# A mixer's small weights loaded into another slot and earlier in the queue, and one exponential placed behind another

## The chip, the cores and the metric

The kernel runs on one core of one Trainium2 chip. The time is that of one whole execution on the device, in microseconds, as the median of several runs; lower is better. The core's engines are TensorE (PE, matrix products), VectorE (DVE), ScalarE (ACT), GpSimd (POOL) and SyncE (SP), which here issues nearly all loads. Each works through its own list of instructions in order and waits on semaphores for the others.

## What is computed

A decoder trunk of two layers on 256 tokens of width 1024. Each layer is a feed-forward with half a step, a mixer, and a second feed-forward; before each stands a root-mean-square norm with its own gain vector. The mixer runs a state-space branch and a gated delta-rule branch on the same input. Cut to what this case touches:

```python
for l in range(DEPTH):
    h = h + 0.5 * swiglu(rms_norm(h, ffn1_norm[l]), ffn1_w_in[l], ffn1_w_out[l])
    u = rms_norm(h, mix_norm[l])
    (z_s, xbc, dt_s, qkv, z_d, b_d, a_d, gate_s, gate_d) = jnp.split(u @ w_in[l], split_points, axis=-1)
    ...
    h = h + merged @ w_out[l]
    h = h + 0.5 * swiglu(rms_norm(h, ffn2_norm[l]), ffn2_w_in[l], ffn2_w_out[l])

dt = jax.nn.softplus(dt_raw + dt_bias)          # state-space branch, 32 heads
a = -jnp.exp(a_log)
beta = jax.nn.sigmoid(b_raw)                    # delta-rule branch, 8 heads
g = -jnp.exp(a_log) * jax.nn.softplus(a_raw + dt_bias)
```

The 48 columns of `w_in` that give `dt_s`, `a_d` and `b_d` are the mixer's small weights. `softplus(x)` is worked out as `max(x, 0) + log(1 + exp(-|x|))`, with the logarithm as a polynomial, so that two exponentials occur in this place: `exp(a_log)` and `exp(-|x|)`.

## The kernel before, in words

**Weights.** All large weights stream through the core as tiles of 128 x 1024 floats (512 KB). A tile is loaded by SyncE into `wraw` (five buffers), and `prep` splits it into a high part `whi` (ScalarE, `act`, line 68) and the rest `wlo` (VectorE, `tt`, line 71), five buffers each. Every product is then three TensorE passes: high by high, high by low, low by high. `take` hands out the next split tile and runs the loads and the splits ahead of it. A split waits until TensorE has done with the tile five before it.

**The order.** The program is written in the order of use. A scheduler puts the instructions of each engine into a list; `tc.issue_after(x)` holds an instruction back in that list until x has been placed, and `state["last"]` is the weight load issued last. `ORDER` lists the units of the mixer: `z` are the products for the gate z_s, `s` the steps of the small scalars, `M` the masks, and so on. `z_unit(0)` comes ahead of the list, and `z20 s z10` begin it. `z_unit` sums in two PSUM banks, one for each half of the tokens (tiles named t), and ScalarE takes each bank off as `yz`.

**Where the mixer begins.** While the feed-forward's last products run, `norm_in` normalises the tokens: `rms_chain` makes `hn` (VectorE, with the gain vector `nw`), TensorE turns it (`hnT`, line 282), and ScalarE and VectorE write it, split, into `uW`. `norm_vec(i)` loads the gain vector of norm i into the single buffer `nw` (line 215). It is called for the next norm before a mixer begins, so this load has to wait until the `hn` of the present norm have read the old vector.

**The small ones.** `mixer` then loads `lp` (convolution weights and two norms, one row for each partition, line 596), `rp` (biases and `a_log`, broadcast, line 598) and `wsr`, the small weights (128 x 8 x 48 floats, line 600). `wsr` lies in `s2`, a pool of nine buffers of 2 KB per partition, through which nearly all temporary tiles of the kernel go in turn. It is split into `wsc` (lines 68 and 71). `scalars`, step one: sixteen narrow matmuls (`psm`, lines 656 to 659), the result copied to `smT` by ScalarE, turned by TensorE (`pst`, line 664), read back as `pvs`, and then the softplus on `scr` by VectorE with ScalarE's tanh and exponential; `ea` is `exp(a_log)`, and `la` their product. Step two multiplies `la` into running sums (`psr`).

**The other slots.** `y0` to `y3` are four slots of 4 KB per partition. In a feed-forward each holds one `wsum`, a sum of two weight tiles, and they are used up one after the other; the fourth, `y3`, is split for the last time ahead of the five last weight tiles. In the mixer `y3` holds `dN` (written by the masks, `M`), and later one of the `yz`.

**Tables.** ScalarE's silu and its exponential need different tables. A table load (ACT_TABLE_LOAD) stands wherever the function changes from one set to another.

Of the kernel before, what the change touches and what calls it, by code (L numbers as in the profile page):

```python
# [7 lines left out]
F32 = mybir.dt.float32  # L8
F32R = mybir.dt.float32r
I32 = mybir.dt.int32  # L10
AF = mybir.ActivationFunctionType
ALU = mybir.AluOpType
# [4 lines left out]
P = 128  # L17
# [5 lines left out]
KT = D // P  # L23
# [3 lines left out]
RPW = 112  # L27
# [26 lines left out]
def trunk_kernel(ctx, tc, x, wst, wsm, norms, lpar, rpar, cst, out):  # L54
    nc = tc.nc
    V, A, G, PE = nc.vector, nc.scalar, nc.gpsimd, nc.tensor

    cpool = ctx.enter_context(tc.tile_pool(name="cpool", bufs=1))
    wpool = ctx.enter_context(tc.tile_pool(name="wpool", bufs=1))
    slots = ctx.enter_context(tc.tile_pool(name="slots", bufs=1))  # L60
    s2 = ctx.enter_context(tc.tile_pool(name="s2", bufs=9))
# [5 lines left out]
    def act(o, i, func=AF.Copy, **kw):  # L67
        return A.activation(out=o, in_=i, func=func, **kw)  # L68

    def tt(o, a, b, op):  # L70
        return V.tensor_tensor(out=o, in0=a, in1=b, op=op)  # L71

    def stt(o, a, s, b, op0, op1):
        return V.scalar_tensor_tensor(out=o, in0=a, scalar=s, in1=b, op0=op0, op1=op1)

    def ts(o, a, s1, op0, sc2=None, op1=None):
        if op1 is None:
            return V.tensor_scalar(out=o, in0=a, scalar1=s1, scalar2=None, op0=op0)
        return V.tensor_scalar(out=o, in0=a, scalar1=s1, scalar2=sc2, op0=op0, op1=op1)
# [7 lines left out]
    def trb(name):  # L87
        return trp.tile([P, 512], F32, tag="tr", name=name)
# [4 lines left out]
    def small(shape, name, bufs=2):  # L93
        return sm.tile(shape, F32, tag=name, name=name, bufs=bufs)
# [54 lines left out]
    state = {"loaded": 0, "prepped": 0, "taken": 0, "last": None, "hold": False, "behind": {}, "late": {}, "first": 0, "turns": {}, "first_chunk": False, "cap": n_forms}  # L149
# [62 lines left out]
    def norm_vec(i):  # L212
        nw = cpool.tile([P, D], F32, tag="nw", name="nw")
        with tc.issue_after(state["last"].ins):
            nc.sync.dma_start(nw[:], norms[i].partition_broadcast(P))
        return [nw[:, n * 512 : (n + 1) * 512] for n in range(2)]
# [375 lines left out]

    def mixer(l, nxt):
        with tc.issue_after(state["last"].ins):
            lp = cpool.tile([P, LPW], F32, tag="lp", name="lp")
            nc.sync.dma_start(lp[:], lpar[l])
            rp = cpool.tile([P, RPW], F32, tag="rp", name="rp")
            nc.sync.dma_start(rp[:], rpar[l].partition_broadcast(P))
            wsr = s2.tile([P, KT, 48], F32, tag="s2", name="wsr")
            nc.sync.dma_start(wsr[:], wsm[l])  # L600
        snw = lp[:, 240:256]
        dnw = lp[:, 256:257]
        alog = rp[:, 40:80]
# [47 lines left out]
        def scalars():  # L651
            psm = trb("psm")
            for kt in range(KT):
                both = wsc[:, kt].rearrange("p o c -> p (o c)")
                if kt < KT - 1:
                    PE.matmul(psm[0:96, 0:S], both, uTh[:, kt, :], start=kt == 0, stop=False)
                PE.matmul(psm[0:48, 0:S], wsc[:, kt, 0], uTl[:, kt, :], start=False, stop=False)
                if kt == KT - 1:
                    PE.matmul(psm[0:96, 0:S], both, uTh[:, kt, :], start=False, stop=True)
            smT = s2.tile([96, S], F32, tag="s2", name="smT")  # L660
            act(smT[:], psm[0:96, 0:S])
            pst = trb("pst")
            for t in range(2):
                PE.transpose(pst[:, t * 96 : (t + 1) * 96], smT[:, t * P : (t + 1) * P], ident[0:96, 0:96])
            pv2 = pst[:, 0:192].rearrange("p (t o c) -> p t o c", t=2, o=2)
            pvs = small([P, 2, 48], "pvs", 1)
            pv = pvs[:]
            act(pv, pv2[:, :, 1])
            tt(pv, pv2[:, :, 0], pv, ALU.add)
            scr = s2.tile([P, 5, 2, 40], F32, tag="s2", name="scr")  # L670
            xb, ax, z, s_, q_ = (scr[:, i] for i in range(5))
            tt(xb, pv[:, :, 0:40], rp[:, None, 0:40].to_broadcast([P, 2, 40]), ALU.add)
            act(dq[:, :, 8:16], pv[:, :, 40:48], AF.Tanh, scale=0.5)
            ts(dq[:, :, 8:16], dq[:, :, 8:16], 0.5, ALU.mult, 0.5, ALU.add)
            ea = small([P, 40], "ea", 1)
            with tc.issue_after(state["input"][0].ins):
                act(ea[:], alog, AF.Exp)
            stt(ax, xb, -1.0, xb, ALU.mult, ALU.max)
            act(z, ax, AF.Exp, scale=-1.0)
            ts(s_, z, 2.0, ALU.add)  # L680
            V.reciprocal(out=s_, in_=s_)
            tt(s_, s_, z, ALU.mult)
            tt(q_, s_, s_, ALU.mult)
            ts(z, q_, 1.0 / 15.0, ALU.mult)
            for d_ in (13.0, 11.0, 9.0, 7.0, 5.0, 3.0):
                stt(z, z, 1.0 / d_, q_, ALU.add, ALU.mult)
            stt(z, z, 1.0, s_, ALU.add, ALU.mult)
            ts(ax, xb, 0.0, ALU.max)
            stt(sp[:], z, 2.0, ax, ALU.mult, ALU.add)
            stt(la[:], sp[:], -1.0, ea[:, None, :].to_broadcast([P, 2, 40]), ALU.mult, ALU.mult)  # L690
            yield
            psr = trb("psr")
            for t in range(2):
                PE.matmul(psr[0:40, t * 256 : (t + 1) * 256], la[:, t, :], UU, start=True, stop=True)
            pr = psr[:].rearrange("p (t c) -> p t c", t=2)
            V.tensor_copy(rows[0:32], pr[0:32, :, 0:P])
            V.tensor_copy(rows[32:40], pr[32:40, :, P : 2 * P])
            nc.sync.dma_start(rdram[:], rows[:].rearrange("p t c -> p (t c)"))
            pac = trb("pac")
            for t in range(2):  # L700
                PE.transpose(pac[:, t * 40 : (t + 1) * 40], rows[:, t, :], ident[0:40, 0:40])
            V.tensor_copy(ac[:], pac[:, 0:80].rearrange("p (t c) -> p t c", t=2))
            V.tensor_copy(dq[:, :, 0:8], ac[:, :, 32:40])
            yield
            psp = trb("psp")
            for c in range(4):
                PE.matmul(psp[:, c * 16 : (c + 1) * 16], SEL[c % 2], dq[:, c // 2, :], start=True, stop=True)
            for a in range(2):
                V.tensor_copy(
                    pq[64 * a : 64 * a + 64].rearrange("p k h c -> p c k h"),  # L710
                    psp[64 * a : 64 * a + 64, 0:64].rearrange("p (c k h a) -> p c k h a", c=4, k=2, h=4)[:, :, :, :, a],
                )
# [484 lines left out]
        def dn_branch():  # L1197
            ps = branch("d", 4, dn_T)
            m = tg[1]
            for t in range(2):  # L1200
                for n in range(2):
                    sl = slice(n * 512, (n + 1) * 512)
                    stt(m[:, t, sl], m[:, t, sl], 1.0, ps[t][n][:], ALU.add, ALU.mult)

        sc, inv, rc = scalars(), invert(), recur()
        units = {"k": k_unit, "q": q_unit, "v": v_unit}
        rests, heads = {}, {}
# [73 lines left out]
    norm_first(nw0)  # L1281
    for l in range(DEPTH):
        ffn(norm_vec(3 * l + 1))
        mixer(l, norm_vec(3 * l + 2))
        add = ffn(norm_vec(3 * l + 3) if l + 1 < DEPTH else None)
    nw = norm_vec(3 * DEPTH)
    for t in range(2):
# [11 lines left out]
        z = small([P, 2], "zz")  # L1299
# [139 lines left out]
```

## Time and profile before

| | |
|---|---|
| median of three runs | 1545.27 us (1545.19, 1545.27, 1546.01) |
| the profiled execution | 1543.84 us |
| its span, first to last instruction | 1542.1 us |
| busy TensorE, VectorE, ScalarE, GpSimd | 1525.1, 1229.8, 949.8, 82.6 us |
| read from memory | 297.72 MB |
| granted TensorE clock over the span | 0.999 |

The profile is of one execution. Times in its rows count from the first instruction. A row of the timeline gives start, duration, engine, line, operation, output and inputs, shapes and count, and in brackets how long the engine had stood idle just before and who ended that. A row of the chain of waits gives start, duration and the work that the end of the program hung on at that time. Rows of one tile give the duration's least, middle and greatest value in ns. Matmuls overlap, so a row of 0.39 us does not keep TensorE for 0.39 us: what counts is the distance between two starts.

### The profile page before, as it was taken

Reading aid. Unit: us, or ns where it says so; the run is one execution under the profiler, and the core shown is the slowest. Engines: PE = TensorE matmul, PEld = TensorE weight load, DVE = VectorE, ACT = ScalarE, POOL = GpSimd, SP = SyncE. Lnnn points to the kernel's source line nnn. Section 1 sums busy time; section 2 is a strip of 40 time slices with the busy share of each in tenths; the row PEclk is TensorE's granted clock in tenths of the full one; section 3 lists DMA queues with packets and bytes.
Section 4 is the critical chain, followed back from the end, with each engine's and each line's share of the span. In section 5 each row is a group of like instructions: output and inputs, shape, how many; then the busy total and the mean of one; then the engine's idle time right before and its main releaser. Section 6 shows DMA issues by size and latency. Waiting matters only on the chain.

```text
span 1542.1 us, 29082 instructions
## 1 busy us (share of the span) xinstructions
PE 1525.1 (99%) x11473; PEld 1385.3 (90%) x11473; DVE 1229.8 (80%) x1859; ACT 949.8 (62%) x1536; POOL 82.6 (5%) x92
## 2 busy tenths in 40 slices
PE   8999999999999999999999999999999999999998
PEld 7999879999988888999899998899998888899997
DVE  5878768967899766789778887689579996678886
ACT  5656667766665645566555566776756666455565
POOL 0000010000000000000100012010000000000010
PEclk9999999999999999999999999999999999999999
DMA  7687765553565556577866687566346555556775
GB/s 272 187 266 227 232 223 174 183 164 112 180 209 172 157 174 191 184 252 217 264 221 227 204 254 238 182 196 186 117 137 204 180 167 187 175 179 191 250 241 156
DMA packets 98831, 305.73 MB, mean 198 GB/s; under 512 B 22837, under 2 KB 23813, under 8 KB 97670
## 3 DMA queue, kind: packets, MB, share of 16 engines
q1 hardware_dynamic: 93796, 290.95, 57.1%
q0 software_dynamic: 4608, 12.58, 5.0%
q8 instruction: 90, 1.47, 0.4%
q14 instruction: 47, 0.39, 0.1%
q10 hardware_dynamic: 290, 0.33, 0.1%
HBM read 297.72 MB, written 1.92 MB: 194 GB/s over the span
## 4 chain that ended last, share of the span: by engine, by line
PE 90%; DVE 3%; ACT 3%; DMA 2%; issue 1%; POOL 0%; SPq 0%; POOLq 0%; ACTq 0%; DVEq 0%
PE fc L346 10%; PE fc L340 9%; PE fc L345 9%; PE t L366 9%; PE o L337 4%; PE o L336 4%; PE o L335 4%; PE f L366 3%; PE b L337 3%; PE b L335 3%; PE b L336 3%; PE p L336 2%; PE p L335 2%; PE p L337 2%; PE xs L340 1%; PE xs L345 1%
## 5 line engine op out<-in xcount | busy, mean ns | idle before, releaser
L71 DVE TENSOR_TENSOR wlo<-wraw,whi 128x1024 fp32r<-128x1024 f32 x488 | 592.2, 1222 | 189.9 <-ACT whi L68 175.4
L68 ACT ACTIVATE whi<-wraw 128x1024 fp32r<-128x1024 f32 x488 | 511.4, 1059 | 266.8 <-PE fc L345 87.3
L346 PE MATMUL fc<-uW,wlo 128*128 128x256 f32 x1280 | 354.9, 277 | 0.0
L340 PE MATMUL fc<-uW,whi 128*128 128x256 f32 x1280 | 354.1, 277 | 0.0
L345 PE MATMUL fc<-uW,whi 128*128 128x256 f32 x1260 | 348.3, 276 | 0.0
L340 PEld LDWEIGHTS fc<-uW,whi 128*128 128x128 f32 x1280 | 240.5, 188 | 0.8
L346 PEld LDWEIGHTS fc<-uW,wlo 128*128 128x128 f32 x1280 | 240.5, 188 | 0.0
L345 PEld LDWEIGHTS fc<-uW,whi 128*128 128x128 f32 x1260 | 236.5, 188 | 0.8
L366 PE MATMUL t<-whi,uW 128*128 128x512 f32 x512 | 165.4, 397 | 0.0
L366 PEld LDWEIGHTS t<-whi,uW 128*128 128x128 f32 x512 | 95.9, 188 | 21.6 <-issue 1.3
L68 ACT ACTIVATE whi<-wsum 128x1024 fp32r<-128x1024 f32 x64 | 68.0, 1062 | 58.7 <-PE fc L345 32.3
L366 PE MATMUL t<-wlo,uW 128*128 128x512 f32 x256 | 100.1, 392 | 0.0
L71 DVE TENSOR_TENSOR wlo<-wsum,whi 128x1024 fp32r<-128x1024 f32 x64 | 78.2, 1222 | 8.3 <-ACT whi L68 5.9
L335 PE MATMUL b<-whi,bh 128*128 128x512 f32 x192 | 76.1, 398 | 0.3 <-ACT bh L68 0.2
L336 PE MATMUL b<-wlo,bh 128*128 128x512 f32 x192 | 75.0, 390 | 0.0
L337 PE MATMUL b<-whi,bl 128*128 128x512 f32 x192 | 74.3, 394 | 0.3 <-DVE bl L71 0.3
L340 PE MATMUL xs<-uW,whi 128*128 128x256 f32 x256 | 72.8, 284 | 0.0
L346 PE MATMUL xs<-uW,wlo 128*128 128x256 f32 x256 | 71.4, 279 | 0.0
L345 PE MATMUL xs<-uW,whi 128*128 128x256 f32 x254 | 70.5, 278 | 0.0
L335 PE MATMUL o<-whi,gh 128*128 128x512 f32 (+1 forms) x160 | 62.0, 388 | 0.0
L337 PE MATMUL o<-whi,gl 128*128 128x512 f32 (+1 forms) x160 | 61.8, 386 | 0.0
L336 PE MATMUL o<-wlo,gh 128*128 128x512 f32 (+1 forms) x160 | 61.7, 386 | 0.0
(337 smaller groups left out, 3301.2 us busy)
## 6 DMA issues: line engine op xcount, KB each, us to landing
wraw<-in_wst_dram SPq DMA_DIRECT2D x504, 512.0 KB, 4.8
wsum<-in_wst_dram SPq DMA_DIRECT2D x16, 512.0 KB, 7.3
wsum<-in_wst_dram POOLq DMA_DIRECT2D x16, 512.0 KB, 8.6
dc<-rdram SPq DMA_DIRECT2D x8, 1024.0 KB, 8.6
nw<-in_norms_dram SPq DMA_DIRECT2D x6, 512.0 KB, 5.3
h<-u POOLq DMA_DIRECT2D x12, 256.0 KB, 6.4
gb<-rdram SPq DMA_DIRECT2D x8, 256.0 KB, 6.1
h<-in_x_dram SPq DMA_DIRECT2D x4, 256.0 KB, 3.7
```

Of the source, the lines that this page charges most:

```text
L68: return A.activation(out=o, in_=i, func=func, **kw)
L71: return V.tensor_tensor(out=o, in0=a, in1=b, op=op)
L335: PE.matmul(ps, lh, rh, start=start, stop=False)
L336: PE.matmul(ps, lh, rl, start=False, stop=False)
L337: return PE.matmul(ps, ll, rh, start=False, stop=stop)
L340: PE.matmul(ps, wh, mh, start=start, stop=False)
L345: PE.matmul(ps, wh, ml, start=False, stop=False)
L346: PE.matmul(ps, wl, mh, start=False, stop=stop)
L366: ins = PE.matmul(ps[t][:], st, mv, start=k0 == 0 and j == 0, stop=k0 == KT - 2 and j == 5)
```

## The change

`wsr` gets the slot `y3` and its load becomes the first of the four; `rp` and `lp` follow; the vector of the next norm is loaded after them, inside `mixer`, instead of ahead of them. The exponential of `a_log` loses its tie to the beginning of the mixer and is tied behind the exponential of the softplus.

```diff
     def mixer(l, nxt):
         with tc.issue_after(state["last"].ins):
+            wsr = slots.tile([P, KT, 48], F32, tag="y3", name="wsr")
+            nc.sync.dma_start(wsr[:], wsm[l])
+            rp = cpool.tile([P, RPW], F32, tag="rp", name="rp")
+            nc.sync.dma_start(rp[:], rpar[l].partition_broadcast(P))
             lp = cpool.tile([P, LPW], F32, tag="lp", name="lp")
             nc.sync.dma_start(lp[:], lpar[l])
-            rp = cpool.tile([P, RPW], F32, tag="rp", name="rp")
-            nc.sync.dma_start(rp[:], rpar[l].partition_broadcast(P))
-            wsr = s2.tile([P, KT, 48], F32, tag="s2", name="wsr")
-            nc.sync.dma_start(wsr[:], wsm[l])
+        nxt = norm_vec(nxt)
...
             ea = small([P, 40], "ea", 1)
-            with tc.issue_after(state["input"][0].ins):
+            stt(ax, xb, -1.0, xb, ALU.mult, ALU.max)
+            with tc.issue_after(act(z, ax, AF.Exp, scale=-1.0).ins):
                 act(ea[:], alog, AF.Exp)
-            stt(ax, xb, -1.0, xb, ALU.mult, ALU.max)
-            act(z, ax, AF.Exp, scale=-1.0)
...
     for l in range(DEPTH):
         ffn(norm_vec(3 * l + 1))
-        mixer(l, norm_vec(3 * l + 2))
+        mixer(l, 3 * l + 2)
```

What it moves is the same in both mixers. On TensorE and GpSimd the order stays as it was. SyncE's list at the beginning of the first mixer, between the weight loads issued during the feed-forward and the eleven that follow (the norm's vector is nw):

```order
 L171 DMA wraw<-in_wst_dram 128x1024 x28
-L596 DMA lp<-in_lpar_dram 128x257
+L596 DMA wsr<-in_wsm_dram 128x384
+L598 DMA rp<-in_rpar_dram 128x112
+L600 DMA lp<-in_lpar_dram 128x257
 L215 DMA nw<-in_norms_dram 128x1024
-L598 DMA rp<-in_rpar_dram 128x112
-L600 DMA wsr<-in_wsm_dram 128x384
 L171 DMA wraw<-in_wst_dram 128x1024 x11
```

The load of wsr goes from behind nw to the front, that of lp from the front to just ahead of nw. ScalarE's list in the same place, from the normalised input (uW) to the second bank of the first z unit (t_2180 and t_2181 are its two banks):

```order
 L68 ACTIVATE uW<-hnT 128x4x128 x2
+L68 ACTIVATE wsc<-wsr 128x8x48
 L68 ACTIVATE yz<-t_2180 128x512
-L68 ACTIVATE whi<-wraw 128x1024
-L68 ACTIVATE wsc<-wsr 128x8x48
-L68 ACTIVATE whi<-wraw 128x1024
-L68 ACT_TABLE_LOAD
-L68 ACTIVATE ea<-rp 128x40
-L68 ACTIVATE whi<-wraw 128x1024
-L68 ACT_TABLE_LOAD
+L68 ACTIVATE whi<-wraw 128x1024 x3
 L68 ACTIVATE yz<-t_2181 128x512
```

The split of the small weights has moved ahead of one yz and one whi, and ea has left with both its table loads; it now stands behind the exponential of the softplus. VectorE's list, from the same uW to the first step of the softplus:

```order
 L71 TENSOR_TENSOR uW<-hnT,uW 128x4x128 x2
-L71 TENSOR_TENSOR wlo<-wraw,whi 128x1024 x2
 L71 TENSOR_TENSOR wsc<-wsr,wsc 128x8x48
-L71 TENSOR_TENSOR wlo<-wraw,whi 128x1024 x5
+L71 TENSOR_TENSOR wlo<-wraw,whi 128x1024 x7
 L71 TENSOR_TENSOR pvs<-pst,pvs 128x96
```

wsc has moved ahead of two wlo.

## The prediction

> **What bounds the kernel now.** I read the page's busy table and its chain of waits first, then the chain cut to the first mixer's opening, then TensorE's rows there beside the same rows of the second mixer.
>
> ```profile
> PE 1525.1 (99%) x11473; PEld 1385.3 (90%) x11473; DVE 1229.8 (80%) x1859; ACT 949.8 (62%) x1536; POOL 82.6 (5%) x92
> PE 90%; DVE 3%; ACT 3%; DMA 2%; issue 1%; POOL 0%; SPq 0%; POOLq 0%; ACTq 0%; DVEq 0%
> ```
>
> TensorE carries nine tenths of the chain. A step on another engine is worth only the time for which TensorE stands still because of it. The chain names the opening of the first mixer, which is where the change works:
>
> ```profile
> 195.68 6.14 DMA wsr<-in_wsm_dram
> ...
> 202.27 1.04 ACT whi L68
> 203.33 1.28 ACT L68
> ...
> 207.73 2.84 ACT whi L68 x3
> 210.57 0.27 ACT smT L68
> ...
> 210.88 0.38 PE pst L664 x2
> ```
>
> Read as a story: the load of the small weights (wsr) lands at 201.82, ScalarE had been waiting for it, then works off whi tiles and table loads, reaches smT late, and TensorE's transpose pst waits for smT. That is 15.2 us of chain (195.68 to 210.88), but not 15.2 us of loss: TensorE multiplied nearly all that time. The loss is read from TensorE's own rows, first mixer and then second:
>
> ```profile
> 209.45 0.28 PE L659 MATMUL psm<-uW,wsc 128*96 128x256 f32 x1
> ...
> 210.02 0.40 PE L366 MATMUL t<-whi,uW 128*128 128x512 f32 x1
> 210.88 0.38 PE L664 MATMUL pst<-cs,smT 96*128 96x96 f32 x2 [0.46 <-ACT smT L68]
> ...
> 971.60 0.40 PE L366 MATMUL t<-whi,uW 128*128 128x512 f32 x1
> 971.84 0.33 PE L664 MATMUL pst<-cs,smT 96*128 96x96 f32 x2
> ```
>
> In the first mixer pst starts 0.86 us after the matmul ahead of it, in the second 0.24 us, which is the ordinary spacing. So the stall is 0.86 - 0.24 = **0.62 us, once in the program**. The ScalarE rows say why only once:
>
> ```profile
> 201.84 0.53 ACT L68 ACTIVATE wsc<-wsr 128x384 fp32r<-128x384 f32 x1 [2.42 <-DMA wsr<-in_wsm_dram]
> ...
> 210.47 0.36 ACT L68 ACTIVATE smT<-psm 96x256 f32<-96x256 f32 x1
> ...
> 962.11 0.52 ACT L68 ACTIVATE wsc<-wsr 128x384 fp32r<-128x384 f32 x1 [1.11 <-DMA wsr<-in_wsm_dram]
> ...
> 971.35 0.38 ACT L68 ACTIVATE smT<-psm 96x256 f32<-96x256 f32 x1 [0.51 <-PE psm L659]
> ```
>
> In the second mixer ScalarE waited 1.11 us for wsr instead of 2.42, was 1.31 us earlier, and then itself stood 0.51 us waiting for psm. The second mixer thus shows what the first looks like with wsr only a little earlier.
>
> **The change part by part.** *The loads.* SyncE's rows in the first mixer, its wait for hn, and the times to landing of lp and, last, of wsr:
>
> ```profile
> 192.88 0.42 SPq L596 DMA_DIRECT2D lp<-in_lpar_dram  x1
> 194.77 0.33 SPq L215 DMA_DIRECT2D nw<-in_norms_dram  x1
> 195.14 0.43 SPq L598 DMA_DIRECT2D rp<-in_rpar_dram  x1
> 195.68 0.38 SPq L600 DMA_DIRECT2D wsr<-in_wsm_dram  x1
> ...
> SPq L215 <- DVE hn L74: 1.4, 1, 1.4
> ...
> DMA to landing us min/median/max: 4.1/4.3/4.5
> ...
> DMA to landing us min/median/max: 4.6/5.4/6.1
> ```
>
> Today nw waits on SyncE until 194.77 (its tile is still read by hn), and rp and wsr stand behind it. The change gives wsr the place of lp, at about 192.9, with nothing that waits in front. Its landing is bounded by 4.1 us (lp, from this very place) and 6.1 us (wsr behind the 512 KB of nw). I take 4.5 us, nearer lp, since the place is lp's and wsr is only half as large again (384 against 257 floats per partition): landing at 197.4, bounds 197.0 and 199.0, against 201.82 now. nw still leaves at 194.77 or shortly after, since it is hn that holds it. The weight loads behind then leave about 1 us earlier, as rp and wsr no longer stand between. lp leaves about 1 us later and is first read here:
>
> ```profile
> L68 ACT ACTIVATE ca<-kk,lp x16: 457/462/530, 238.2 to 1024.7; 128x256 f32<-128x256 f32 x16
> ```
>
> At 238.2 us, 40 us after it lands: no cost. If that cover were gone, the cost would be the 1 us.
>
> *The slot.* y3's former tenant, the fourth wsum, is worked off in the feed-forward before the last five weight tiles; its next tenant, dN, is written after the masks' loads. Neither holds anything. The tiles that follow wsr in s2 now take a slot that came free one tenant earlier, so their waits can only shorten. I cost both at zero.
>
> *wsc moved forward.* This is the one part that can hurt. ScalarE and VectorE now do wsc ahead of the yz and whi, and ahead of the two wlo, that used to precede it. Should wsr be late, these wait. Prices of wsc and of a wlo, with the two points at which TensorE needs the two wlo:
>
> ```profile
> L68 ACT ACTIVATE wsc<-wsr x2: 524/526/527, 201.8 to 962.1; 128x384 fp32r<-128x384 f32 x2
> L71 DVE TENSOR_TENSOR wsc<-wsr,wsc x2: 559/559/559, 202.4 to 962.7; 128x384 fp32r<-128x384 f32 x2
> ...
> 199.46 1.23 DVE L71 TENSOR_TENSOR wlo<-wraw,whi 128x1024 fp32r<-128x1024 f32 x1 [0.99 <-ACT whi L68]
> ...
> 202.47 0.39 PE L366 MATMUL t<-wlo,uW 128*128 128x512 f32 x1
> ...
> 203.84 0.39 PE L366 MATMUL t<-wlo,uW 128*128 128x512 f32 x1
> ```
>
> With landing at 197.4, wsc ends on ScalarE at 197.9 and on VectorE at 198.5; the first wlo ends at 199.7 and the second, two wlo after wsc, at about 201.0. TensorE reads them at 202.47 and 203.84. The slack is some 2.7 us, so wsr may take up to 4.5 + 2.7 = 7.2 us. The longest wsr seen took 6.1. Cost: zero.
>
> *The exponential.* ea moves behind the exponential of z, where the right table is in place. Two table loads of 1.28 us go per mixer, four in all, 5.1 us of ScalarE, and ScalarE stops waiting 2.42 and 1.11 us for wsr. What remains is that ScalarE, which reached smT at 210.47, 0.74 us after psm was done (209.45 + 0.28), reaches it early, so the 0.62 us stall goes. In the second mixer the same gain falls into ScalarE's idle time.
>
> ```profile
> 203.33 1.28 ACT L68 ACT_TABLE_LOAD   x1
> 204.63 0.24 ACT L68 ACTIVATE ea<-rp 128x40 f32<-128x40 f32 x1
> ...
> 220.18 0.24 DVE L74 SCALAR_TENSOR_TENSOR la<-sp,ea 128x80 f32<-128x80 f32 x1
> ```
>
> ea costs 0.24 us and is read at 220.18 only; behind z (ScalarE at 213.93 today) it still has some 6 us. If that cover were gone it would cost 0.24 us each time.
>
> The Trainium skill, in "ScalarE: Activation LUTs", section "What ACT_TABLE_LOAD costs", has a switch at 1283 ns for the load and about 1380 ns for a drain, 2.66 us together. The load agrees with the 1.28 us row; no drain of that size shows around it here, as ea starts 1.30 us after the load started. By the page ScalarE would gain 10.6 us instead of 5.1, and the sum of TensorE's time below would be the same, while the rival of freed ScalarE time would be larger.
>
> *The sum.* 0.62 us in the first mixer, 0 in the second. The profiled execution took 1543.84 us, 1542.1 of it the span; less 0.62 that is 1543.2. The median shown lies 1.43 us above that execution; carried over, 1545.27 - 0.62 = **1544.65 us**, 0.04% faster. About 0.2% (3.1 us) can be told from no change, so this counts as no change.
>
> **The rivals.** *Nothing is left of it.* The two mixers as wholes, from the first matmul of one to the feed-forward's first:
>
> ```profile
> 190.50 4.12 PE t L366 x18
> ...
> 597.10 4.12 PE f L366 x18
> ...
> 952.08 4.12 PE t L366 x18
> ...
> 1359.00 4.12 PE f L366 x18
> ```
>
> The first takes 406.60 us with the stall, the second 406.92 without it. A gain of 0.62 us is thus within what later stretches give and take; eaten up, the time is 1545.3. Against it: every engine downstream is fed by the same TensorE order, so that a shift has no reason to be lost.
>
> *Freed ScalarE time is worth more.* If ScalarE set the pace from here on, its four table loads (5.1 us) and its waits for wsr (2.42 + 1.11) would come off: 8.6 us, 1536.6. For it speaks that the chain runs through ScalarE for over 5 us in the rows quoted first; against it that ScalarE is busy 62% and that the second mixer turned 1.31 us of such time into 0.51 us of waiting and none of TensorE's. Something above 3.1 us would need a stall that these rows do not show.
>
> The page on ScalarE named above would add four drains of 1.38 us to this rival: 14.1 us and 1531.1; the row of 1.30 us speaks against that.
>
> *wsr lands late and stops TensorE: slower.* Place: wsc at the head of ScalarE and VectorE, with the two wlo behind it; it decides from 7.2 us to landing. The worst landing of another 512 KB load from this queue, nw, is in this row:
>
> ```profile
> DMA to landing us min/median/max: 3.6/5.3/9.5
> ```
>
> At 9.5 us each mixer would stand 2.3 us: 2 x 2.3 - 0.6 = 4.0 us, 1549.3. Against it: wsr is 192 KB, its longest is 6.1, and ahead of it stand the same weight loads that let lp land within 4.5.
>
> **How the numbers follow.** The stall goes and the gain stays: 0.62. Nothing is left: 0.20. Freed ScalarE time: 0.10. wsr late: 0.08. The first two lie within 0.2%, so 0.82 for no change, 0.10 faster, 0.08 slower. The range covers the first two with the scatter of the runs (1545.19 to 1546.01, and 1543.84 under the profile), which reaches some 1.4 us to either side, and leaves out most of the two others: 1542.5 to 1547.0.
>
> **What would show it.** Right: wsr issued near 192.9 and 954.4 us, landing in under 7 us; wsc on ScalarE just after uW; smT waiting for psm in both mixers; pst 0.24 us behind its neighbour in both; two table loads fewer per mixer; the feed-forward after the first mixer starting 0.6 us earlier, the second mixer of unchanged length. Wrong: a gap of TensorE at the first wlo of the second z unit (wsr late), a mixer shorter by more than 1 us (freed ScalarE time matters somewhere I did not see), or a new stall far behind, at the masks or the decays.

## The result, and the profile after

The changed kernel took 1542.88 us in the median of 17 runs, the kernel before, beside it, 1545.19 us (17 runs): a ratio of 0.9985, 95% interval 0.9978 to 0.9992. That is 2.3 us or 0.15% faster, inside the 0.2% that the prediction called no change, and inside its range. But the forecast gain was 0.62 us. Two more comparisons, below, gave 0.9997 (0.9989 to 1.0006) and 0.9988 (0.9979 to 0.9997); the mean of the three is 0.9990, some 1.5 us. The question left by the result is thus the size.

The page of the changed kernel, its span and its chain by engine:

```profile
span 1539.7 us, 29072 instructions
PE 89%; DVE 4%; ACT 2%; DMA 2%; issue 1%; SPq 1%; POOL 0%; POOLq 0%; ACTq 0%; DVEq 0%
```

Nothing in these shares tells of the change; the opening of the mixers does. First SyncE's rows, then ScalarE's, then TensorE's, of the first mixer after the change (line numbers behind the mixer's loads are one higher):

```profile
191.94 0.43 SPq L596 DMA_DIRECT2D wsr<-in_wsm_dram  x1
192.41 0.42 SPq L598 DMA_DIRECT2D rp<-in_rpar_dram  x1
192.88 0.43 SPq L600 DMA_DIRECT2D lp<-in_lpar_dram  x1
193.83 0.33 SPq L215 DMA_DIRECT2D nw<-in_norms_dram  x1
```

```profile
197.00 0.53 ACT L68 ACTIVATE wsc<-wsr 128x384 fp32r<-128x384 f32 x1 [1.33 <-DMA wsr<-in_wsm_dram]
197.43 0.58 ACT L68 ACTIVATE yz<-t 128x512 f32<-128x512 f32 x1
...
206.99 1.06 ACT L68 ACTIVATE whi<-wraw 128x1024 fp32r<-128x1024 f32 x1 [0.27 <-PE t L366]
208.83 0.38 ACT L68 ACTIVATE smT<-psm 96x256 f32<-96x256 f32 x1 [0.78 <-PE psm L660]
...
210.50 1.28 ACT L68 ACT_TABLE_LOAD   x1
211.79 0.27 ACT L68 ACTIVATE scr<-scr 128x80 f32<-128x80 f32 x1
211.97 0.22 ACT L68 ACTIVATE ea<-rp 128x40 f32<-128x40 f32 x1
```

```profile
209.09 0.40 PE L366 MATMUL t<-whi,uW 128*128 128x512 f32 x1
209.32 0.33 PE L665 MATMUL pst<-cs,smT 96*128 96x96 f32 x2
```

wsr leaves as soon as the weight loads ahead of it have left, at 191.94 where 192.9 was forecast (all rows of this execution come 0.9 us earlier, see below), lands 5.0 us later (forecast 4.5, bounds 4.1 and 6.1), and ScalarE now stands 0.78 us idle before smT, waiting for psm, where it had come late. pst starts 0.23 us after its neighbour: the stall of 0.62 us is gone, and ea runs at once behind scr with no table load of its own. In the second mixer pst had no stall before and has none now. So the mechanism did what was forecast. That leaves 1.7 us of the 2.4 between the spans of these two executions, 1542.1 and 1539.7 us, unexplained by it, and TensorE's rows show where they lie: 0.9 us in the first 15 us of the program, where nothing was changed, 0.2 us elsewhere in the first mixer and 0.6 us in the second. At the start TensorE's matmuls of 512 columns follow one another every 0.43 us, later every 0.23; the faster spacing begins near 15.2 us before the change and near 13.3 after it, which makes up the 0.9 us.

### The profile page after: what moved, and what is told of

It is laid out like the page before. It is cut to its first block, busy times and chain, and to the rows that moved or that the text cites. A ratio compares the mean times of both kernels' runs of the same rounds, so it can differ in the third digit from the quotient of the medians.

```text
span 1539.7 us, 29072 instructions
## 1 busy us (share of the span) xinstructions
PE 1522.8 (99%) x11473; PEld 1384.4 (90%) x11473; DVE 1229.7 (80%) x1859; ACT 944.8 (61%) x1532; POOL 81.8 (5%) x92
## 4 chain that ended last, share of the span: by engine, by line
PE 89%; DVE 4%; ACT 2%; DMA 2%; issue 1%; SPq 1%; POOL 0%; POOLq 0%; ACTq 0%; DVEq 0%
PE fc L346 10%; PE fc L340 9%; PE fc L345 9%; PE t L366 9%; PE o L337 4%; PE o L335 4%; PE o L336 4%; PE f L366 3%; PE b L335 3%; PE b L337 3%; PE b L336 3%; PE p L336 2%; PE p L337 2%; PE p L335 2%; PE xs L345 1%; PE xs L340 1%
```

## The experiments

Theory A: only the stall of 0.62 us counts, the rest is scatter. Theory B: the change has a second gain of about 1.7 us. The first four kernels ran on one chip: the two kernels again, and each half of the change alone.

**The kernel before, unchanged.**

> The kernel before, unchanged, timed against itself, to see what the comparison itself can tell. Both theories: ratio 1.000 within 0.0007 (about 1 us). Trace: the stall ahead of pst in the first mixer is there again (0.86 us between its start and the start ahead), none in the second (0.24). Theory A (only the stall matters; all else between the first two traces was scatter): TensorE's slower stretches and its slow start of up to 15 us lie elsewhere than in the first trace, by some tenths of a us each. Theory B (the change has a second gain of some 1.7 us): the differences to the changed kernel's trace at the start and in the second mixer come back in the same places.

Ratio 1.0002 (0.9993 to 1.0010). But the stall was another one. ScalarE's wait for wsr and TensorE's pst in the first mixer of this execution:

```profile
202.09 0.52 ACT L68 ACTIVATE wsc<-wsr 128x384 fp32r<-128x384 f32 x1 [3.66 <-DMA wsr<-in_wsm_dram]
```

```profile
209.03 0.40 PE L366 MATMUL t<-whi,uW 128*128 128x512 f32 x1
211.13 0.38 PE L664 MATMUL pst<-cs,smT 96*128 96x96 f32 x2 [1.71 <-ACT smT L68]
```

The distance is 2.10 us instead of 0.86, so the stall is 1.86 us, three times that of the first profile. wsr took 7.4 us to land instead of 6.1, ScalarE waited 1.24 us longer, and the stall is 1.24 us longer. The same kernel, in another execution: neither theory had foreseen this.

**The changed kernel again.**

> The changed kernel once more, beside the others on one chip. Theory A: 0.6 to 0.7 us under the kernel before (ratio 0.9996). Theory B: 2.3 us under it (0.9985). Trace: pst 0.24 us behind its neighbour in both mixers, wsr landing 5 us after its issue.

Ratio 0.9997 (0.9989 to 1.0006): too wide to part 0.62 from 1.5 us, but it holds no 2.3. pst stood 0.23 us behind its neighbour in both mixers.

**The loads alone.** The changed kernel with the old place of the exponential:

```diff
-            stt(ax, xb, -1.0, xb, ALU.mult, ALU.max)
-            with tc.issue_after(act(z, ax, AF.Exp, scale=-1.0).ins):
+            with tc.issue_after(state["input"][0].ins):
                 act(ea[:], alog, AF.Exp)
+            stt(ax, xb, -1.0, xb, ALU.mult, ALU.max)
+            act(z, ax, AF.Exp, scale=-1.0)
```

> The changed loads alone, with the exponential of a_log tied as before: its two table loads then stand right behind wsc, ahead of the first yz and of three whi (2 x 1.28 + 0.24 = 2.8 us more on ScalarE at that place). Theory A: the stall ahead of pst goes (-0.62 in the first mixer), but the second wlo of the second z unit ends about 0.3 us after TensorE wants it, in both mixers: sum about 0 (-0.62 + 2 x 0.3). Theory B: the second gain hangs on the loads or on the freed ScalarE time; 1 us or more faster if on the loads.

Ratio 0.9992 (0.9983 to 1.0001). The stall at pst is gone in both mixers (0.23), and the small new one is there in the first mixer, in TensorE's rows at the second wlo of the second z unit:

```profile
203.97 0.62 PE L366 MATMUL t<-whi,uW 128*128 128x512 f32 x2
204.64 0.50 PE L366 MATMUL t<-wlo,uW 128*128 128x512 f32 x1
204.98 0.62 PE L366 MATMUL t<-whi,uW 128*128 128x512 f32 x2
```

The row of two starts at 203.97 and 204.20. The next start, due 0.23 us later, comes after 0.44, and the one behind it after 0.34: 0.32 us lost in all, the 0.3 that was expected. But it was expected in both mixers, and the second lost less than 0.1 us.

**The exponential alone.** The kernel before with only the second half of the diff (the lines above with their signs exchanged).

> The moved exponential alone, with slot and order of the loads as before: wsc still waits for wsr until 201.8 us in the first mixer, but two table loads (2.6 us) are gone behind it. Theory A: that alone is more than the 0.74 us by which ScalarE was late for smT, so the stall goes: -0.62 us, as much as with the whole change, so that the two halves do not add up. Theory B: a part of 2.3 us that adds up with the other half.

Ratio 0.9988 (0.9979 to 0.9997). ScalarE's rows:

```profile
201.28 0.53 ACT L68 ACTIVATE wsc<-wsr 128x384 fp32r<-128x384 f32 x1 [3.41 <-DMA wsr<-in_wsm_dram]
...
208.20 0.38 ACT L68 ACTIVATE smT<-psm 96x256 f32<-96x256 f32 x1 [0.78 <-PE psm L659]
```

wsr lands as late as ever, with a wait of 3.41 us, and smT is in time all the same. Each half of the change takes the whole stall away, and the halves do not add up. Against theory B speaks that neither half shows a gain which the other lacks, as far as intervals of 0.0009 to either side can tell.

From here the theory is C: the stall is ScalarE's wait for wsr less 1.80 us, and it changes with the landing of wsr from execution to execution. The next four kernels, on another chip, test it.

**The kernel before, a third time.**

> The kernel before once more. Theory C (new: the stall ahead of pst is as long as ScalarE's wait for wsr less 1.80 us, and that wait changes from execution to execution with the landing of wsr): wait 2.42 gave a stall of 0.62, wait 3.66 one of 1.86 (2.10 less the ordinary 0.24); this trace must give wait less 1.80 in the first mixer again, and none in the second as long as the wait there is under 1.8. Rival (the stall has another cause, such as the table loads): no such relation. Ratio 1.000 within 0.0008.

Ratio 1.0000 (0.9991 to 1.0009). ScalarE and TensorE, first mixer:

```profile
202.97 0.53 ACT L68 ACTIVATE wsc<-wsr 128x384 fp32r<-128x384 f32 x1 [3.07 <-DMA wsr<-in_wsm_dram]
```

```profile
212.01 0.39 PE L664 MATMUL pst<-cs,smT 96*128 96x96 f32 x2 [1.12 <-ACT smT L68]
```

pst came 1.51 us after its neighbour, a stall of 1.27 us; 3.07 - 1.80 = 1.27. Behind the law stands a fixed piece of ScalarE's list: pst starts 9.04 us after wsc in all three executions (201.84 and 210.88, 202.09 and 211.13, 202.97 and 212.01).

**The changed kernel, a third time.**

> The changed kernel once more, for the size of the gain. Theory C: the mean of the stalls seen so far in the first mixer of the kernel before (0.62 and 1.86) is 1.2 us, so a ratio near 0.9992; pst 0.24 us behind its neighbour in both mixers whatever the landing. Theory A (always 0.62): 0.9996. Theory B (2.3 us): 0.9985.

Ratio 0.9988 (0.9979 to 0.9997), pst 0.24 and 0.23 us behind its neighbour, with landings of 4.2 and 4.8 us. Theory C's 0.9992 is inside, theory B's 0.9985 too, theory A's 0.9996 just so.

**wsr later by four weight tiles**, in the kernel before:

```diff
             wsr = s2.tile([P, KT, 48], F32, tag="s2", name="wsr")
-            nc.sync.dma_start(wsr[:], wsm[l])
...
         z_unit(0, None)
+        with tc.issue_after(state["last"].ins):
+            nc.sync.dma_start(wsr[:], wsm[l])
```

> The kernel before with the load of wsr issued four weight tiles later, so some 9 us later (about 205 us in the first mixer, 965 in the second); everything else kept, but the scheduler puts wsc and ea elsewhere to match. It lands at 210 to 212 and 970 to 972, wsc is done 1.1 us later, and psm wants it at 207.7 and 969.3. Theory C: TensorE stands at psm 3.5 to 5 us in the first mixer and 2 to 3.5 in the second, in place of the stall at pst: 4 to 7 us slower in all, each us of lateness one us of time. Rival (TensorE makes up for stalls later, since other engines set the pace behind): less than half of that.

Ratio 1.0010 (1.0000 to 1.0021), 1.6 us slower by the medians. TensorE's first psm of the first mixer:

```profile
207.84 0.63 PE L366 MATMUL t<-whi,uW 128*128 128x512 f32 x2
210.71 0.33 PE L657 MATMUL psm<-uW,wsc 128*96 128x256 f32 x1 [2.25 <-DVE wsc L71]
```

psm came 2.65 us after its neighbour, and 1.68 in the second mixer: stalls of 2.42 and 1.45 us, 3.9 in all where 5.5 to 8.5 were expected, since SyncE sent wsr off at 202.9 and not at 205. Less the stall at pst that they replace (1.3 us on average, as it came out) some 2.6 us were to be lost; the measured 1.6 has that within its interval (0 to 3.2 us). By its number alone the result is nearer to what the rival expected; what parts them is TensorE's rows, where the stalls are, and the smaller lateness of wsr.

In this execution the first stall cost more than its length. TensorE before it and with it, behind it, and later (time, TensorE busy with its matmuls counted, granted clock, DMA share, GB/s):

```profile
207.00:211.00 4.00, 1.75 (x9) 1.00 0.91 318
211.30:214.60 3.30, 3.30 (x15) 0.50 0.52 160
214.70:225.00 10.30, 10.30 (x47) 1.00 0.35 117
```

Behind the stall TensorE ran at half its clock for more than 3 us. The first 315 matmuls of this mixer took 57.4 us, against 53.3 to 53.4 in five profiles without a stall: 4.1 us lost, 2.4 of them by standing still. With the 1.5 us of the second mixer that is 5.6 us, within the 5.5 to 8.5 expected, though not for the reason given. The median does not show it: the mean granted clock is 0.998 in this execution and 0.999 or 1.000 in the nine others, so the half clock seems to belong to this one, and the sum for the median leaves it out.

**wsr late, but wsc held ahead as in the change**: the slower rival of the prediction.

```diff
-            nc.sync.dma_start(wsr[:], wsm[l])
...
         nxt = norm_vec(nxt)
+        with tc.issue_after(state["last"].ins):
+            nc.sync.dma_start(wsr[:], wsm[l])
...
-            act(wsc[:, :, 0], wsr[:])
-            tt(wsc[:, :, 1], wsr[:], f(wsc[:, :, 0]), ALU.subtract)
+            state["behind"][state["taken"] + 1] = [act(wsc[:, :, 0], wsr[:]).ins]
+            state["late"][state["taken"]] = tt(wsc[:, :, 1], wsr[:], f(wsc[:, :, 0]), ALU.subtract)
```

> The changed kernel with the load of wsr behind that of the next norm's vector again, and with wsc held ahead of the three whi and of all wlo that follow, as in the change. This is the slower rival of the prediction. wsr lands 6 to 7.4 us after its issue, near 202 and 962 to 964 us; the first wlo is then done 2.3 us after the landing. Theory C: TensorE stands at its first use of that wlo 1.7 to 3.0 us in the first mixer and 0.5 to 1.5 in the second, none at pst: 2.2 to 4.5 us above the changed kernel, 0 to 3 us above the kernel before (ratio 1.000 to 1.002). Rival (the split weights made ahead cover it): as the changed kernel.

Ratio 1.0015 (1.0006 to 1.0024). ScalarE, then TensorE at the first wlo of the second z unit:

```profile
202.46 0.53 ACT L68 ACTIVATE wsc<-wsr 128x384 fp32r<-128x384 f32 x1 [4.28 <-DMA wsr<-in_wsm_dram]
```

```profile
202.65 0.62 PE L366 MATMUL t<-whi,uW 128*128 128x512 f32 x2
204.76 0.50 PE L366 MATMUL t<-wlo,uW 128*128 128x512 f32 x1 [1.49 <-DVE wlo L71]
```

The wlo is ready 2.3 us after wsr landed (202.46 to 204.76), as the prediction had it from single durations, and TensorE stood 1.66 us there and 0.45 in the second mixer. At pst, where no stall was expected, it stood 0.2 and 0.5 us: in the first mixer the last whi ahead of smT had waited 1.40 us for its weight tile. That is 2.8 us of stalls; the medians of this chip lie 2.3 us above the kernel before and 4.5 us above the changed kernel, the latter at the upper end of what was expected.

The last two kernels, on a third chip, part the slot from the order of the loads.

**The slot alone**: the kernel before with wsr in `slots`, `tag="y3"`.

> The kernel before with wsr in the slot y3, everything else kept (order of the loads, ea). wsr no longer waits 0.3 us for the turned hn, but still for nw ahead of it. Theory C: the slot by itself is worth nothing: ScalarE waits 1.1 to 3.7 us for wsr, and the stall in the first mixer is that wait less 1.80, as in the kernel before: ratio 1.000 within 0.001. Rival (the shifted turns of the pool s2 take waits away elsewhere): 1 us or more faster with the stall still there.

Ratio 1.0002 (0.9991 to 1.0013). ScalarE and TensorE, first mixer:

```profile
202.68 0.52 ACT L68 ACTIVATE wsc<-wsr 128x384 fp32r<-128x384 f32 x1 [3.28 <-DMA wsr<-in_wsm_dram]
```

```profile
211.72 0.39 PE L664 MATMUL pst<-cs,smT 96*128 96x96 f32 x2 [1.33 <-ACT smT L68]
```

pst came 1.73 us after its neighbour, a stall of 1.49 us: the law holds a fourth time (3.28 - 1.80 = 1.48), and the slot shows no gain.

**The changed kernel without the slot**: wsr in `s2` again.

> The changed kernel with wsr back in s2. Its load is first in SyncE's queue but has to wait until TensorE has turned hn, near 195.6 us by the first profile, and rp, lp, nw and the weights wait behind it. It lands 4 to 5 us later, near 200, about 3 us later than in the changed kernel. Theory C: ScalarE waits some 4 us at wsc, but the first wlo is done 2.3 us after the landing, just when TensorE wants it, and ea's table loads are gone: no stall at pst, at most 0.5 us at that wlo in the first mixer: ratio near that of the change, 0.999 to 1.000. Rival (the slot is what matters): the stall of the kernel before is back, ratio 1.000 or above.

Ratio 0.9979 (0.9970 to 0.9989). The expectation was wrong at one point, in this kernel's SyncE rows:

```profile
188.50 3.85 SPq L171 DMA_DIRECT2D wraw<-in_wst_dram  x2
192.41 0.42 SPq L596 DMA_DIRECT2D wsr<-in_wsm_dram  x1
```

wsr left at once, some 3 us before TensorE had turned the last hn in this execution (195.5), so its buffer in s2 was free by then. No stall at pst or at a wlo. The new slot is thus no condition of the gain: place in the queue and place of the exponential are.

## Why the prediction was right, and what was off

- **The bound.** That only TensorE's standstill counts, and that 15 us of chain through wsr and ScalarE hold less than 1 us of it in that execution, held. That the second mixer would keep its length did not: it was 0.6 us shorter, away from the opening, where TensorE's pace changes from execution to execution (below).
- **The mis-sized term.** The step "0.62 us in the first mixer, 0 in the second" took one execution for the kernel. The stall ahead of pst was 0.62, 1.86, 1.27 and, with the slot alone, 1.49 us in four profiles, a mean of 1.31 us, and the first profile happened to be the least of them. Its bounds should have come from wsr's landing, which the prediction itself gave a spread. With 1.31 the sum is 1545.27 - 1.31 = 1543.96 us, a ratio of 0.9992, which lies in or on the edge of each of the three intervals. The three kernels that do without the stall by other means had 0.9992, 0.9988 and 0.9979; the three that keep it 1.0002, 1.0000 and 1.0002.
- **What stays open.** Between the 1.3 us that the stalls explain and the 1.5 us that three comparisons gave on average lies no more than the scatter of either. But the changed kernel without the slot was 3.2 us faster (0.9979), and its interval (0.9970 to 0.9989) leaves 1.3 us out. Part of this is the kernel before on that chip, four of whose 19 executions show a mean granted clock of 0.998 and average 1548.3 us. The mean of the other 15 is 1545.2 us, and the ten of the kernel without the slot, none of them below 0.999, average 1543.0: 2.3 us. What the rest is, and whether theory B has something in it after all, stays open; so the cause of the stall is shown, and its size in the median only to about a microsecond.
- **The loads.** Landing of 3.9 to 5.2 us in the changed kernel (5.5 once without the slot) against 4.6 to 7.4 in the old place; forecast 4.5 with bounds of 4.1 and 6.1. TensorE's rows show no stall that lp, rp or nw caused.
- **The slot.** Costed at zero; alone it left the stall where it was and showed no gain (1.0002, 0.9991 to 1.0013).
- **wsc ahead.** The slack of 2.7 us rested on a wlo 2.3 us after the landing; the kernel with the late load showed these 2.3 us and the price behind them. The changed kernel never came near (longest landing 5.2 us, against the 7.2 from which it would lose).
- **The exponential.** Its two table loads, together 2.6 us per mixer, are alone more than ScalarE was late. The Trainium skill ("ScalarE: Activation LUTs", "What ACT_TABLE_LOAD costs") adds a drain of about 1380 ns to each load. No trace here shows it: in the changed kernel the load at 210.50 takes 1.28 us and scr starts 0.01 us behind it.
- **The rivals.** "Nothing is left of it" falls by the first and the third comparison, while the second (0.9997) could not exclude it; the second mixer's length changes with TensorE's pace (below). "Freed ScalarE time is worth more" falls: the exponential alone frees the four table loads and gained 1.8 us (0.9988), not 5.1. "wsr lands late" is real as a mechanism and does not happen.

## What to carry to other kernels

Where a stall hangs on a transfer's landing, one profile gives one draw of it: find the fixed piece of work behind the landing (here 9.04 us from wsc to pst), and price the stall over the spread of landings. Two cures of one wait do not add up; try each alone before both are kept. Look at the granted clock behind a long standstill too: it can cost more than its length. A small load that an engine will wait for belongs ahead of the large one that nobody needs yet.

## What the runs showed of the hardware

**Scatter.** The scatter of this kernel between executions lies mostly in the mixers and the first 15 us. From the first product of the feed-forward behind the first mixer to the first product of the second mixer TensorE took 354.98 us in each of the twelve profiles; a mixer took 405.75 to 410.18 us, stalls included.

**A second pace.** Part of it is TensorE's pace: in some stretches of 10 to 30 us its matmuls follow one another about 4% more slowly, with the granted clock at 1.00 all the while. The same window of the second mixer in the kernel before, first profile and then its repetition (columns as above):

```profile
1070.00:1080.00 10.00, 10.00 (x87) 1.00 0.71 221
```

```profile
1070.00:1080.00 10.00, 10.00 (x91) 1.00 0.72 234
```

87 matmuls against 91, with the same clock and somewhat less traffic beside the slower. The repetition is 1 us later in its program here, so the surer comparison is of the same work: the 85 matmuls that begin at 1070.02 us in the first profile took 10.01 us in three of the twelve profiles and 9.63 us in the nine others. What sets the slower pace was not tried.

**Half the clock.** Two of the twelve traces have a stretch of some 3.4 us at a granted clock of 0.50 in the middle of the program. One is shown above (wsr later by four weight tiles); the other is in the second mixer of the slot-alone kernel, where TensorE had waited for a tile of VectorE's:

```profile
1172.99 1.22 PE L1045 MATMUL cbb<-BC 128*128 128x256 f32 x2 [3.00 <-DVE vb L71]
```

```profile
1172.40:1175.80 3.40, 2.81 (x8) 0.50 0.09 35
```

TensorE's standstills ahead of them, 2.25 and 3.00 us, are the longest of all twelve traces (start and end of the program left out); the next longest, 1.71 us, was not followed by such a stretch. That the standstill is the cause was not tried. Among all the executions timed with their clock, traced or not, the mean granted clock was below 0.999 in 20 of 117 executions of the kernels that keep the stall at pst and 3 of 71 of those without it. On average the 20 were 2.4 to 3.2 us longer than the other executions of their kernel on the same chip. Whether the stall makes them more frequent was not tried either.

**Landing.** The landing of wsr, 192 KB from the same place of the same queue, took 6.1, 7.4, 6.8, 7.1 and 7.0 us in the first mixer of five executions, and 4.6 to 5.4 in the second. Why it is longer in the first was not tried.
